# Writing the exponentials of a tile's second part in place in SBUF instead of into a PSUM bank

## The chip, the core and the metric

The kernel runs on one core of one Trainium2 chip. The metric is the device time of one execution in microseconds. Three runs of the kernel before gave 1191.39, 1193.56 and 1194.45 us; the median is 1193.56 us. Lower is better.

## What is computed

The program is a two-layer decoder trunk on 1024 tokens of width 1024. Only the second layer's main branch matters here: attention with a forget gate, 16 heads of width 64, causal, over keys and values that are projected once. In the reference, cut to what matters:

```python
logits = jnp.einsum('bqhd,bkhd->bhqk', qi, k) * scale
logits = logits + (ci[..., :, None] - cum_k[:, :, None, :])
logits = jnp.where(mask[None, None], logits, -jnp.inf)
p = jax.nn.softmax(logits, axis=-1)
return jnp.einsum('bhqk,bkhd->bqhd', p.astype(v.dtype), v)
```

The queries go through in blocks of 128. `cum` is the running sum of the log forget gates; in the kernel it comes as a row `R` that is added to the logits.

## The kernel before

The stage is `fox`. It runs 16 heads one after the other (head 0 to head 15), and in each head eight tiles of 128 queries, the longest first: tile 7 has 1024 keys, tile 0 has 128. A tile with more than 512 keys goes in two parts: 512+512 (tile 7), 512+384 (tile 6), 512+256 (tile 5), 384+256 (tile 4). Tiles 3 to 0 have one part.

The texts below use one letter for each step of a tile, with the tile's number and `a` or `b` for its part. All of it stands in `probs`, `inverse_of` and `halves`:

- **The logits**: two TensorE matmuls (L323) into a PSUM bank of tag `L`, of which there are three.
- **R**: the VectorE reduction on L1028. It reads the `L` bank, adds the row, writes the sum to the SBUF tile `p` (tag `MK`, four slots) and keeps the running minimum. When it has read the bank, the matmuls may use that bank again.
- **E**: the exponential on ScalarE (L1036). It reads `p`, writes `e`, and gives the row's sum. Its bias is the minimum over both parts, so E of part `a` too must wait until R of part `b` is done.
- **S** and **V**: the sum of the parts' sums (L1046, or L1048 for one part) and its reciprocal (L1049), on VectorE.
- **C**: on ScalarE (L1064), `e` times the reciprocal, rounded to float16, into the tile `P`.
- **H**: on VectorE (L1065), the rest that the rounding left: `e` times the reciprocal minus C's result, into the other half of `P`.

The two halves are then transposed by a DMA (L1081) and meet the values on TensorE (L1090) six tiles later. C and H of a tile are written in the program behind the first R of the next tile.

`e` lies in a PSUM bank of tag `T`. There are two such banks, and in the kernel before each part of a tile takes one. So a tile of two parts takes both, and E of the next tile waits for H of this one.

Between these steps run pieces of the projections for the coming heads: matmuls on L359, which fill most of TensorE's time, and their evacuations, which share VectorE and ScalarE with the steps above (L912 and L913 queries and keys, L816 and L817 values, L375 and L376 gates, L1107 and L1108 the output of the values). GpSimd adds the causal mask to the row (L1002) and scales and splits the projection weights (L176, L193, L178). During heads 14 and 15 the weights of the output projection are split too (L198 on ScalarE, L199 on VectorE, L193 on GpSimd).

TensorE's order is the program's order, fixed by hand. The order on VectorE and ScalarE is made by the scheduler from what each instruction needs and from which slots are free; so is most of GpSimd's and of the DMA queue's.

Of the kernel before, what the change touches and what calls it, by code (L numbers as in the profile page):

```python
# [18 lines left out]
P = 128  # L19
# [4 lines left out]
NH = 512  # L24
# [54 lines left out]
def trunk_kernel(ctx, tc, x, xT, memT, win, wk, wv0, wv, wmk, wmv, wout, poolw, pscale, lng, lnb, bforget, out):  # L79
# [20 lines left out]
    def nm(tag):  # L100
        count[0] += 1
        return f"{tag}{count[0]}"
# [4 lines left out]
    def ps(shape, tag, bufs):  # L107
        return psum.tile(shape, F32, tag=tag, name=nm(tag), bufs=bufs)
# [7 lines left out]
    def MK(shape, dt=F32R):  # L116
        return sb(list(shape), "MK", 4, dt)
# [7 lines left out]
    def tiny(n, dt=F32):  # L125
        return small.tile([P, n], dt, tag=f"s{n}{dt}", name=nm("s"), bufs=4 if n < 12 else 2)
# [193 lines left out]
    def mm3(acc, terms):  # L320

        for i, (a, b) in enumerate(terms):
            nc.tensor.matmul(acc, a, b, start=i == 0, stop=i == len(terms) - 1)  # L323
# [137 lines left out]
    def mem_attention(l, X, kv, qtile, ytile, yd, behind=None, before=None, last=None):  # L461
# [61 lines left out]
        with tc.manual_schedule(engines={PE}):  # L523
            for t in range(ST + 2):
                part = fill.left / (ST + 2 - t)
                if t < ST:
                    probs(t)
                if before and t == ST - 2:
                    before()
                if last and t == ST:  # L530
                    last(0)
                at = (0.3, 0, 0.1, 0.6) if t in (5, 9) else (1, 0, 0, 0)
                for h in range(MH):
                    fill.pump(part * at[h])
                    if t in (5, 9):
                        values((t - 5) // 4, h)
            fill.pump(float("inf"))
# [258 lines left out]
    with tc.tile_pool(name="in1", bufs=1) as in1:  # L796
# [194 lines left out]
        def parts_at(i):  # L991

            L = (i + 1) * P
            return [(0, L)] if L <= NH else [(0, 384), (384, L)] if L == 640 else [(0, NH), (NH, L)]
# [17 lines left out]
        def probs(hd, i, R, sums, inverse, behind):  # L1012

            q, kx, ky = pairs[hd // 2][hd % 2]
            qs = slice(i * P, (i + 1) * P)
            p = MK([P, S], F32)  # L1020
            C, parts = diagonal.pop((hd, i)), parts_at(i)
            m = tiny(2)
            top = -NEG
            for n, (lo, up) in enumerate(parts):
                lg = ps([P, NH], "L", 3)[:, : up - lo]
                mm3(lg, ((q[:, qs], kx[:, lo:up]), (q[:, qs], ky[:, lo:up])))
                rows = C[:, : up - lo] if n == len(parts) - 1 else R[:, lo:up]
                nc.vector.tensor_tensor_reduce(p[:, lo:up], lg, rows, unq, top, ALU.add, ALU.min, m[:, n : n + 1])  # L1028
                top = m[:, n : n + 1]
                if n == 0:  # L1030
                    inverse()
            behind()
            es = []
            for n, (lo, up) in enumerate(parts):
                e = ps([P, NH], "T", 2)[:, : up - lo]
                nc.scalar.activation(  # L1036
                    e, p[:, lo:up], AF.Exp, bias=top, scale=-1.0, accum_out=sums[:, n, hd % 2, i : i + 1],
                )
                es.append((lo, up, e))
            return hd, i, es, sums  # L1040
# [92 lines left out]
        def fox(following, out_proj, head):  # L1133
# [8 lines left out]
            for hd in range(HEADS + 1):  # L1142
# [16 lines left out]
                for i in range(ST if hd < HEADS else LAG):  # L1159
# [37 lines left out]
                    if hd < HEADS:  # L1197
                        new = (hd, tile_of, o)
                        fresh[0] = probs(hd, tile_of, R, sums, inverse, behind)
                    else:  # L1200
                        inverse()
                        behind()
                        out_proj.split(11 + i, True, gp_copy)
                        if i > 1:
                            out_proj.fetch_two(two_lines(4 + 2 * i))
# [91 lines left out]
```

## Time and profile before

| | |
|---|---|
| the profiled execution, its own time | 1193.68 us |
| its span, first to last instruction | 1192.0 us |
| median of the runs | 1193.56 us (1191.39 to 1194.45) |
| mean granted TensorE clock | 0.998 |
| stage of the 16 heads | about 645 to 1055 us of the span |
| VectorE, ScalarE, GpSimd busy in the whole span | 783.0, 684.9, 286.0 us |

The span is what the trace covers; 1.68 us of the profiled execution lie around it. A row of the timeline gives the start, the duration, the engine, the line and the operation, then what is written and read with sizes; a bracket at the end gives how long the engine had sat idle and what ended that. A row with x2 or more stands for so many instructions, and its shape is the first one's. Busy times and waits are averages over very different stretches, so the trace is read here head by head.

### The profile page before, as it was taken

What the parts mean: (1) busy time and instruction counts of PE and PEld (TensorE: products, weight loads), DVE (VectorE), ACT (ScalarE), POOL (GpSimd) and SP (SyncE); (2) the same over time, 40 slices, a digit from 0 to 9 for tenths busy, and PEclk for the clock granted to TensorE, in tenths of its full rate; (3) what the DMA queues carried; (4) which work ended last, traced back from release to release, by engine and by line L of the source; (5) the groups of instructions that cost most, each with busy time, mean ns of one, the idle gap of its engine ahead of it and who ended that gap; (6) DMA issues with size and microseconds to landing.
All of it is one profiled execution on the core that took longest, in us unless ns stands there. A gap on an engine that the chain in (4) does not pass through costs nothing. (4 is left out here: it accounts for less than half of the span.)

```text
span 1192.0 us, 19788 instructions
## 1 busy us (share of the span) xinstructions
PE 1164.5 (98%) x6893; PEld 672.4 (56%) x6941; DVE 783.0 (66%) x1840; ACT 684.9 (57%) x1512; POOL 286.0 (24%) x437
## 2 busy tenths in 40 slices
PE   9999999999999999999999999999999999999996
PEld 5566776555555557556574555555555545455553
DVE  6744675555765566447655888778877788884654
ACT  6568775966563234557431776666766677674210
POOL 3321001310000000000002454555555444750000
PEclk9999999999999999999999999999999999999999
DMA  7576656754286544446634889989996899964530
GB/s 258 179 237 194 162 113 213 239 182 145 91 281 174 144 133 119 140 130 124 173 150 113 173 183 218 192 170 201 193 216 145 167 193 208 238 164 171 176 108 35
DMA packets 286195, 203.88 MB, mean 171 GB/s; under 512 B 224912, under 2 KB 238352, under 8 KB 286096
## 3 DMA queue, kind: packets, MB, share of 16 engines
q1 hardware_dynamic: 279696, 181.59, 60.9%
q0 software_dynamic: 6400, 21.04, 5.4%
q8 instruction: 54, 0.88, 0.3%
q14 instruction: 45, 0.37, 0.1%
HBM read 116.01 MB, written 22.61 MB: 116 GB/s over the span
## 5 line engine op out<-in xcount | busy, mean ns | idle before, releaser
L359 PE MATMUL pj<-A,w 128*128 128x512 f16 (+2 forms) x2874 | 660.8, 382 | 3.3 <-DMA A<-A 0.9
L359 PEld LDWEIGHTS <-w 128*128 128x128 f16 (+1 forms) x2560 | 245.5, 98 | 278.4 <-issue 9.9
L1036 ACT ACTIVATE T<-MK,s 128x512 f32<-128x512 f32 x192 | 111.2, 579 | 66.0 <-DVE s L1028 48.8
L1065 DVE SCALAR_TENSOR_TENSOR P<-T,s,P 128x512 f16<-128x512 f32 x192 | 112.0, 613 | 39.4 <-ACT P L1064 38.3
L1064 ACT ACTIVATE P<-T,s 128x512 f16<-128x512 f32 x192 | 102.9, 576 | 53.5 <-issue 28.9
L599 PEld LDWEIGHTS <-T 128*128 128x128 bf16 x736 | 70.6, 98 | 89.5 <-issue 4.4
L1002 POOL TENSOR_SCALAR_AFFINE_SELECT raw<-R 128x256 f32<-128x256 f32 (+3 forms) x128 | 59.8, 469 | 185.5 <-DVE s L1028 102.8
L323 PE MATMUL L<-A 128*128 128x512 f16 (+3 forms) x384 | 84.7, 326 | 5.5 <-DVE s L1028 5.4
L199 DVE TENSOR_TENSOR w<-raw,w 128x512 bf16<-128x512 f32 x74 | 51.8, 701 | 54.1 <-ACT w L198 38.8
L885 POOL MEMSET G<- 128x128 f32 x1 | 0.2, 204 | 335.2 <-DVE V L541 335.2
L359 PEld LDWEIGHTS pj<-A,w 128*128 128x128 f32 x352 | 65.2, 188 | 16.9 <-ACT w L198 1.5
L199 DVE TENSOR_TENSOR T<-T,T 128x1024 bf16<-128x1024 f32 x23 | 28.1, 1220 | 71.0 <-PE pj L599 37.9
L323 PEld LDWEIGHTS <-A 128*128 128x128 f16 x384 | 37.4, 98 | 48.9 <-issue 7.6
L178 POOL TENSOR_TENSOR w<-B,w 128x512 f16<-128x512 f32 x54 | 63.2, 1172 | 4.0
L198 ACT CAST T<-T 128x1024 fp32r<-128x1024 f32 x23 | 24.1, 1047 | 64.7 <-DMA T<-y1d 34.6
L198 ACT CAST w<-raw 128x512 fp32r<-128x512 f32 x76 | 46.7, 615 | 23.8 <-DMA raw<-in_win_dram 10.7
L1090 PEld LDWEIGHTS <-V 128*64 128x64 f16 (+1 forms) x1152 | 50.6, 104 | 13.3 <-issue 5.6
L1090 PE MATMUL O<-T,V 128*64 128x128 f16 (+1 forms) x1152 | 57.5, 220 | 0.4 <-ACT T L1036 0.4
L599 PE MATMUL pj<-B,T 128*128 128x512 bf16 (+1 forms) x187 | 52.1, 385 | 0.3
L1028 DVE CUSTOM_DVE_ANT_0 MK<-L,R,scales 128x512 f32<-128x512 f32 x64 | 45.3, 708 | 9.7 <-PE L L323 9.3
L200 ACT CAST w<-raw 128x512 bf16<-128x512 f32 x78 | 48.2, 618 | 5.7 <-PE pj L359 4.3
L599 PE MATMUL L<-B,T 128*128 128x512 bf16 (+1 forms) x165 | 46.9, 394 | 0.4 <-ACT T L200 0.2
(286 smaller groups left out, 1845.7 us busy)
## 6 DMA issues: line engine op xcount, KB each, us to landing
raw<-in_win_dram SPq DMA_DIRECT2D x66, 256.0 KB, 3.5
W<-in_win_dram POOLq DMA_DIRECT2D x48, 256.0 KB, 4.1
R<-cumd SPq DMA_DIRECT2D x16, 512.0 KB, 4.5
B<-in_win_dram SPq DMA_DIRECT2D x15, 512.0 KB, 5.1
y0d<-Y SPq DMA_DIRECT2D x12, 512.0 KB, 4.2
raw<-in_wout_dram SPq DMA_DIRECT2D x24, 256.0 KB, 2.7
T<-y0d SPq DMA_DIRECT2D x12, 512.0 KB, 4.9
A<-A SPq DMA_DIRECT2D x24, 256.0 KB, 3.9
```

The costliest lines, as they stand in the source:

```text
L178: pin(nc.gpsimd.tensor_tensor(to.lo, src, to.hi, ALU.subtract))
L198: pin(nc.scalar.copy(to.hi, src))
L199: pin(nc.vector.tensor_tensor(to.lo, src, to.hi.bitcast(F32), ALU.subtract))
L200: pin((top or nc.scalar.copy)(to.top, src))
L323: nc.tensor.matmul(acc, a, b, start=i == 0, stop=i == len(terms) - 1)
L359: nc.tensor.matmul(accs[n], a[:, k, :], b[:, pc * 4 + k, n * NH : (n + 1) * NH], start=seen[n] == 1, stop=seen[n] == 3 * KT,)
L599: nc.tensor.matmul(accs[a][nh], y, w, start=kt == 8 and i == 0, stop=kt == 7 and i == 2,)
L1002: tc.keep_in_program_order(nc.gpsimd.affine_select(C[:, :w], R[:, lo:up], [[-1, w]], ALU.is_ge, -NEG, base=w - P, channel_multiplier=1,))
L1036: nc.scalar.activation(e, p[:, lo:up], AF.Exp, bias=top, scale=-1.0, accum_out=sums[:, n, hd % 2, i : i + 1],)
L1064: nc.scalar.activation(pair[:, lo:up], e, AF.Copy, scale=r)
L1065: nc.vector.scalar_tensor_tensor(pair[:, L + lo : L + up], e, r, pair[:, lo:up], ALU.mult, ALU.subtract)
L1090: nc.tensor.matmul(acc[rows, (i % 4) * P : (i % 4) * P + P], v[:, b, 2 * j : 2 * j + (1 if e else 2), :].rearrange("p e d -> p (e d)"), pt ...
```

## The change

`e` of a tile's first part still goes into a `T` bank; `e` of the second part is written over `p` in SBUF:

```diff
             es = []
             for n, (lo, up) in enumerate(parts):
-                e = ps([P, NH], "T", 2)[:, : up - lo]
+                e = p[:, lo:up] if n else ps([P, NH], "T", 2)[:, : up - lo]
                 nc.scalar.activation(
                     e, p[:, lo:up], AF.Exp, bias=top, scale=-1.0, accum_out=sums[:, n, hd % 2, i : i + 1],
                 )
```

No instruction is added or removed. For the four tiles of two parts in each head, 64 in all, E of part `b` writes SBUF, and C and H of part `b` read SBUF. A tile now takes one `T` bank, and `p` stays in use until H of its part `b`. TensorE's rows are the same ones in the same order. On ScalarE and VectorE the scheduler makes another order.

ScalarE at the start of head 7, before. The tile `p` is `MK_8938` for tile 7 and `MK_8981` for tile 6; L1036 is E, L1064 is C, L1107 evacuates the output of the values:

```order
L1036 ACTIVATE T_8953,sums_8561<-MK_8938,s_8939 128x512
L1036 ACTIVATE T_8955,sums_8561<-MK_8938,s_8939 128x512
L1064 ACTIVATE P_8994<-T_8953,s_8987 128x512
L1064 ACTIVATE P_8994<-T_8955,s_8987 128x512
L1107 ACTIVATE G_8560<-O_9005,scales 64x512
L1036 ACTIVATE T_8999,sums_8561<-MK_8981,s_8982 128x512
L1036 ACTIVATE T_9001,sums_8561<-MK_8981,s_8982 128x384
```

The same place with the change (`p` is `MK_8910` for tile 7, `MK_8952` for tile 6, `MK_9037` for tile 5):

```order
L1036 ACTIVATE T_8925,sums_8537<-MK_8910,s_8911 128x512
L1036 ACTIVATE MK_8910,sums_8537<-MK_8910,s_8911 128x512
L1036 ACTIVATE T_8970,sums_8537<-MK_8952,s_8953 128x512
L1064 ACTIVATE P_8965<-T_8925,s_8958 128x512
L1064 ACTIVATE P_8965<-MK_8910,s_8958 128x512
L1036 ACTIVATE MK_8952,sums_8537<-MK_8952,s_8953 128x384
L1107 ACTIVATE G_8536<-O_8975,scales 64x512
L1036 ACTIVATE T_9055,sums_8537<-MK_9037,s_9038 128x512
```

E6a has moved ahead of C7a and C7b, and E5a stands right behind L1107. Heads 0 to 3, 6, 7 and 10 to 13 have this order with the change; heads 4, 5, 8, 9, 14 and 15 keep E7a, E7b, C7a, C7b, E6a.

VectorE a little later in head 7, before (L1065 is H of tile 7, then L1108, R5a, S6, R5b):

```order
L1065 TENSOR_SCALAR P_8994<-T_8953,s_8987,P_8994 128x512
L1065 TENSOR_SCALAR P_8994<-T_8955,s_8987,P_8994 128x512
L1108 TENSOR_SCALAR G_8560<-O_9005,scales,G_8560 64x512
L1028 ISA MK_9067,s_9068<-L_9069,R_8601,scales 128x512
L1046 TENSOR_SCALAR s_9073<-sums_8561 128x1
L1028 ISA MK_9067,s_9068<-L_9076,raw_8900,s_9068,scales 128x256
```

And with the change:

```order
L1065 TENSOR_SCALAR P_8965<-T_8925,s_8958,P_8965 128x512
L1065 TENSOR_SCALAR P_8965<-MK_8910,s_8958,P_8965 128x512
L1028 ISA MK_9037,s_9038<-L_9039,R_8576,scales 128x512
L1108 TENSOR_SCALAR G_8536<-O_8975,scales,G_8536 64x512
L1046 TENSOR_SCALAR s_9043<-sums_8537 128x1
L1028 ISA MK_9037,s_9038<-L_9046,raw_8872,s_9038,scales 128x256
```

R5a and L1108 have changed places, and H7b reads two SBUF tiles (`MK` and `P`) where it read a PSUM bank and one SBUF tile.

VectorE at the start of head 14, before (R7a, L817, R7b, then H0a of head 13, R6a, S7, R6b, V7):

```order
L1028 ISA MK_11591,s_11592<-L_11600,raw_11464,s_11592,scales 128x512
L1065 TENSOR_SCALAR P_11561<-T_11564,s_11597,P_11561 128x128
L1028 ISA MK_11639,s_11640<-L_11641,R_11255,scales 128x512
L1046 TENSOR_SCALAR s_11645<-sums_11583 128x1
L1028 ISA MK_11639,s_11640<-L_11648,raw_11519,s_11640,scales 128x384
L1049 RECIPROCAL s_11645<-s_11645 128x1
```

And with the change:

```order
L1028 ISA MK_11535,s_11536<-L_11544,raw_11408,s_11536,scales 128x512
L1046 TENSOR_SCALAR s_11588<-sums_11527 128x1
L1049 RECIPROCAL s_11588<-s_11588 128x1
L1028 ISA MK_11582,s_11583<-L_11584,R_11202,scales 128x512
L1065 TENSOR_SCALAR P_11595<-T_11550,s_11588,P_11595 128x512
L1028 ISA MK_11582,s_11583<-L_11591,raw_11463,s_11583,scales 128x384
```

R6a now stands behind S7 and V7, and R6b behind H7a; H0a of the head before has gone ahead of R7a. Heads 4 and 8 change in the same way; heads 5, 9 and 15 had this order already.

## The prediction

> **What bounds the kernel now.** I read the page's first part, then the busy time of the stage of the 16 heads as one stretch, then who waited for whom in that stretch, TensorE first. The rows are:
>
> ```profile
> PE 1164.5 (98%) x6893; PEld 672.4 (56%) x6941; DVE 783.0 (66%) x1840; ACT 684.9 (57%) x1512; POOL 286.0 (24%) x437
> 640.00:1060.00 420.00, 414.10 (x2886) 218.55 (x2886) 327.48 (x937) 286.53 (x681) 217.94 (x327) 1.00 0.91 191
> PE L L323 <- DVE s L1028: 5.4, 8, 2.1
> PE O L1090 <- ACT T L1036: 0.4, 1, 0.4
> DVE P L1065 <- ACT P L1064: 38.3, 61, 1.1
> DVE MK L1028 <- PE L L323: 9.3, 7, 4.3
> ACT T L1036 <- DVE P L1065: 16.6, 42, 0.8
> ```
>
> The second row has, behind the 420 us, the busy times of TensorE, its weight loads, VectorE, ScalarE and GpSimd. TensorE is busy for 414.1 of 420 us, so the whole stage holds 5.9 us that could be won: eight waits of logits matmuls for R (5.4 us) and one at the values (0.4). VectorE has 22% idle, but the waits say what kind: it stands for ScalarE's C (38.3 us) and almost never for TensorE (9.3 us in only 7 places). VectorE and ScalarE hand each tile back and forth, R, E, S, V, C, H, and this loop, not their busy time, runs close behind TensorE. The wait that the change removes, E for H's bank, is 16.6 us of ScalarE's time. It costs TensorE only where it makes an R late.
>
> The eight places, one row each from the timeline:
>
> ```profile
> 702.68 0.38 PE L323 MATMUL L<-A 128*128 128x256 f16 x2 [0.23 <-DVE s L1028]
> 726.07 0.38 PE L323 MATMUL L<-A 128*128 128x256 f16 x2 [0.54 <-DVE s L1028]
> 828.67 0.38 PE L323 MATMUL L<-A 128*128 128x256 f16 x2 [0.44 <-DVE s L1028]
> 931.27 0.38 PE L323 MATMUL L<-A 128*128 128x256 f16 x2 [0.45 <-DVE s L1028]
> 971.44 0.48 PE L323 MATMUL L<-A 128*128 128x384 f16 x2 [0.26 <-DVE s L1028]
> 978.80 0.38 PE L323 MATMUL L<-A 128*128 128x256 f16 x2 [1.12 <-DVE s L1028]
> 1024.82 0.48 PE L323 MATMUL L<-A 128*128 128x384 f16 x2 [0.30 <-DVE s L1028]
> 1034.41 0.38 PE L323 MATMUL L<-A 128*128 128x256 f16 x2 [2.05 <-DVE s L1028]
> ```
>
> The 256-wide ones are the logits of tile 4, part b, in heads 2, 3, 7, 11, 13 and 15; they need the bank that R5a frees, three banks back. The 384-wide ones are those of tile 6, part b, in heads 13 and 15, and need R7a.
>
> **The new order, walked through head 7.** I take durations from the trace and the new order from the rows shown with the change.
>
> ```profile
> 820.51 0.74 DVE L1028 CUSTOM_DVE_ANT_0 MK<-L,R,scales 128x512 f32<-128x512 f32 x1
> 822.62 0.69 ACT L1036 ACTIVATE T<-MK,s 128x512 f32<-128x512 f32 x1 [1.93 <-DVE s L1028]
> 823.34 0.67 ACT L1036 ACTIVATE T<-MK,s 128x512 f32<-128x512 f32 x1
> 824.18 0.21 DVE L1046 TENSOR_SCALAR s<-sums 128x1 f32<-128x1 f32 x1 [0.92 <-ACT T L1036]
> 824.33 0.68 DVE L1028 CUSTOM_DVE_ANT_0 MK<-L,raw,s 128x384 f32<-128x384 f32 x1
> 824.93 0.16 DVE L1049 RECIPROCAL s<-s 128x1 f32<-128x1 f32 x1
> 825.17 1.26 ACT L1064 ACTIVATE P<-T,s 128x512 f16<-128x512 f32 x2 [1.03 <-issue]
> 825.89 1.41 DVE L1065 SCALAR_TENSOR_TENSOR P<-T,s,P 128x512 f16<-128x512 f32 x2 [0.80 <-ACT P L1064]
> 827.22 0.73 DVE L1108 SCALAR_TENSOR_TENSOR G<-O,scales,G 64x512 f32<-64x512 f32 x1
> 827.88 0.73 DVE L1028 CUSTOM_DVE_ANT_0 MK<-L,R,scales 128x512 f32<-128x512 f32 x1
> ```
>
> Before: R6b ends at 825.01, C7a starts at 825.17, H7a 0.72 later, both H take 1.41, L1108 follows, and R5a ends at 828.61; TensorE goes on at 828.67. With the change ScalarE has E6a ahead of C7a, and E6a needs the minimum that R6b completes: it starts at 825.05, and since one E follows another after 0.72 (822.62 to 823.34), C7a starts at 825.77 instead of 825.17. H7a starts at 825.77 + 0.72 = 826.49, both H are over at 827.90, and R5a, which no longer stands behind L1108, runs from 827.82 (neighbours overlap by 0.07) to 828.55. So at this place the change gives 0.66 (L1108 out of the way) and takes 0.60 (E6a in the way): **0.06 us, nearly nothing**. ScalarE's wait for the bank is gone, and TensorE's stall here stays, unless the head starts earlier.
>
> The gain comes later in the head, from tile 4:
>
> ```profile
> 834.23 1.14 DVE L1065 SCALAR_TENSOR_TENSOR P<-T,s,P 128x512 f16<-128x512 f32 x2 [0.80 <-ACT P L1064]
> 835.01 0.58 ACT L1036 ACTIVATE T<-MK,s 128x384 f32<-128x384 f32 x1 [0.45 <-DVE P L1065]
> 837.35 1.01 DVE L1065 SCALAR_TENSOR_TENSOR P<-T,s,P 128x384 f16<-128x384 f32 x2 [0.70 <-ACT P L1064]
> 843.90 0.74 DVE L1028 CUSTOM_DVE_ANT_0 MK<-L,R,scales 128x512 f32<-128x512 f32 x1
> 818.32 1.03 PE L323 MATMUL L<-A 128*128 128x512 f16 x4
> 841.83 1.03 PE L323 MATMUL L<-A 128*128 128x512 f16 x4
> ```
>
> E4a waited here until H5a gave its bank back (835.01). With the change that bank was freed by H6a, and E4a stands behind E5b, at about 832.3; S4 is then ready before H5a, and H4a can start at about 836.6, 0.75 earlier. Of this the next head keeps some 0.45, since H0a (about 0.3) now stands ahead of its R7a: R7a of head 8 at about 843.45, not 843.90. One turn of the loop takes 22.95 us instead of the 23.39 from 820.51 to 843.90. TensorE's own turn is 841.83 - 818.32 = 23.51 with its stall of 0.44, so 23.1 without.
>
> **The cost of reading SBUF.** The moved operations have no row before; the nearest ones:
>
> ```profile
> L1065 DVE SCALAR_TENSOR_TENSOR P<-T,s,P 128x512 f16<-128x512 f32 x80 | 58.8, 748 | 28.9 <-ACT P L1064 27.9
> L172 DVE SCALAR_TENSOR_TENSOR w<-raw,scales,w 128x512 f16<-128x512 f32 x22 | 16.2, 748 | 9.5 <-ACT w L171 9.4
> L504 ACT ACTIVATE P<-P,s 128x256 f16<-128x256 f32 x64 | 27.3, 497 | 3.7 <-ACT P L498 2.6 <-DVE s L502 1.0
> L1064 ACT ACTIVATE P<-T,s 128x256 f16<-128x256 f32 x48 | 22.3, 465 | 2.9 <-ACT T L1036 2.8
> L199 DVE TENSOR_TENSOR MK<-raw,MK 128x512 bf16<-128x512 f32 x8 | 5.5, 688 | 9.6 <-ACT MK L198 9.5
> L199 DVE TENSOR_TENSOR MK<-A,MK 128x512 bf16<-128x512 f32 x4 | 4.3, 1091 | 0.1
> ```
>
> H by itself costs the same: 748 ns with a PSUM and an SBUF input, 748 ns with two SBUF inputs (L172). C costs 32 ns more from SBUF (497 against 465), 64 times on ScalarE, 2 us in all beside idle time. E into SBUF I take as free. But L199, with two SBUF inputs, takes 688 ns early and 1091 ns in head 14 and behind it, where GpSimd is busier: up to 0.40 us more. H of part b becomes such an instruction, while GpSimd is busy for 217.94 of 420 us, 52%. So one H costs between 0 and 0.40 more; I take 0.52 x 0.40 = 0.2, four times a head, 0.8, and let half of it vanish in VectorE's waits, which remain. The turn is then 22.95 + 0.4 = 23.35, against 23.39 before in head 7: at the middle of the bounds the price eats what the order gives.
>
> The Trainium skill speaks against the change here: SBUF — State Buffer, section "Who interferes with whom", says that a VectorE instruction with two SBUF inputs and a GpSimd one that reads SBUF block each other, while one with a single SBUF input does not contend. The 688 and 1091 ns of L199 agree; by a full block at every H the sum would come out as in the second rival below. The skill's Perfetto Trace Analysis, section "Optimizing Scalar/DVE Operations", puts VectorE's access at some 60 ns from SBUF and 125 ns from PSUM; by that H would be 65 ns cheaper, which the equal 748 ns do not show.
>
> **The sum.** Against the profiled execution, 1193.68 us, of which 1192.0 is span. What the loop's turn is worth shows best where heads of the new order follow each other:
>
> ```profile
> 898.64 0.75 DVE L1028 CUSTOM_DVE_ANT_0 MK<-L,R,scales 128x512 f32<-128x512 f32 x1 [0.68 <-PE L L323]
> 970.63 0.74 DVE L1028 CUSTOM_DVE_ANT_0 MK<-L,R,scales 128x512 f32<-128x512 f32 x1
> ```
>
> These are R7a of heads 10 and 13: 72.0 us for three heads, 24.0 each. At 23.35, plus 0.35 in head 10, which starts up to date and waits for TensorE's tiles, it is 70.4, so head 13 starts 1.6 earlier. TensorE itself comes 0.45 earlier (head 11's stall), so 1.15 of head 13's 0.26 + 1.12 goes. Head 6 starts up to date as well, so heads 7 and 11 lose their 0.44 and 0.45. Of heads 2 and 3 (0.23 + 0.54) I take 0.5. Head 15 keeps its 0.30 + 2.05: its order is the old one up to tile 4, and head 14 ahead of it gets the order R7b, S7, V7, R6a, in which R5a comes about 2 us later (R6a, 0.66, no longer fills VectorE's wait for E7b, and S6, which waits for E6a and E6b, 1.5, stands ahead of R5a). For that order in heads 4, 8 and 14 I set 0.3 of new stalls. Gain: 0.44 + 0.45 + 1.15 + 0.5 - 0.3 = 2.2 us. The execution would take 1191.5; the median of the runs lies 0.12 below the profiled one, so **1191.3 us**.
>
> **The rivals.**
>
> *The loop loosens everywhere.* Head 14 and 15 profit too and the eight waits all go. For it: 16.6 us of E's waits fall away, three times what TensorE loses. Against it: the orders of heads 14 and 15. The ceiling is 5.9 us: 1193.56 - 5.8 = 1187.8.
>
> *GpSimd's hold on SBUF decides.* H of part b costs the full 0.40 each and half or all of it lands in the loop, 0.8 to 1.6 a head: turns of 23.75 to 24.55 against TensorE's 23.1. In the ten heads of the new order TensorE would lose 0.65 to 1.45 a head, less some 1.2 that a run of heads starts with in hand (R7a of head 7 came 820.51 - 818.32 = 2.2 behind its logits and stalled 0.44; a head that is up to date has about 0.6), three runs: 6.5 - 3.6 = 3 to 14.5 - 3.6 = 11, and 1.5 more in heads 14 and 15. With head 15's 2.35 and the 0.4, the stalls are 7 to 15 instead of 5.9: 1195 to 1203, nearest 1197. It decides from about 0.15 us an H that is not absorbed.
>
> *Given back at the end.* Heads 2 to 13 gain 2.2, and the later R5a of head 14 makes head 15 start 2 us later: 1193.5.
>
> That the change does not do what it says is excluded by the order: 64 E write the `MK` tile. The longer life of `p` costs no wait: even where only two of its four slots are left, in head 15, R of a tile stands behind H of the tile two before it in VectorE's own order.
>
> **Chances.** The forecast has 0.38, its own range 1189.6 to 1192.8. All waits gone, 0.20; GpSimd decides, 0.30; given back, 0.12. For 8 in 10 the range runs from 1187.6 to 1197.6: it holds the forecast, the ceiling and the nearer half of the GpSimd rival. 0.3% of the time is 3.6 us, about what a measurement of this kernel can tell from no change. Faster by more (below 1190.0): 0.10 of the forecast and the whole first rival, 0.30. Slower by more (above 1197.1): 0.25 of the GpSimd rival and 0.02 of the last, 0.27. Within: 0.43.
>
> **What would show it.** Right: E no longer waits for L1065; the 256-wide waits of heads 7, 11 and 13 shrink below 0.3 while head 15's stays near 2; H of part b (P<-MK) 0.1 to 0.3 us longer than H of part a at 512. Wrong: H of part b at 1.0 us or more; TensorE's waits for R above 6 us in sum; C7a not delayed by E6a; TensorE's waits for R below 1 us.

## The result and the profile after

The changed kernel takes 1196.84 us (median of six runs, 1195.68 to 1198.35), the kernel before 1193.13 (six runs, 1191.23 to 1194.45). The ratio is 1.0033, with a 95% interval of 1.0020 to 1.0047: **slower by about 3.7 us**, where 2.2 us less had been forecast. The profiled execution took 1198.35 us, with a span of 1196.6.

The page's first part, and the busy times of the stage of the 16 heads (TensorE, its weight loads, VectorE, ScalarE, GpSimd), after:

```profile
PE 1169.4 (98%) x6941; PEld 672.3 (56%) x6941; DVE 788.0 (66%) x1840; ACT 685.3 (57%) x1512; POOL 294.6 (25%) x437
640.00:1060.00 420.00, 412.78 (x2876) 217.01 (x2874) 328.81 (x933) 285.38 (x678) 222.28 (x323) 1.00 0.90 188
```

VectorE and GpSimd are each some 5 to 9 us busier over the span with the same instructions. Who waited for whom in the stage, after:

```profile
ACT T L1036 <- DVE P L1065: 3.8, 11, 1.0
ACT T L1036 <- DVE s L1028: 97.2, 86, 2.7
DVE P L1065 <- ACT P L1064: 35.9, 56, 1.4
PE L L323 <- DVE s L1028: 4.8, 8, 1.1
PE L L323 <- DVE s L1049: 1.7, 2, 1.2
```

E's wait for the bank that H frees has shrunk from 16.6 to 3.8 us, as meant. It bought nothing: E waits for R instead, 97.2 us where it was 48.8. TensorE's waits for R are 4.8 us against 5.4, and a wait of another kind is new (1.7 us, logits that start a head). The profile puts it down to a V (L1049); `e1` and `e12` below, in which the moves of the queries come earlier, are without it. The places of the timeline where TensorE stood idle in the stage and right behind it (two of 0.38 and 0.34 us for evacuations left out), after:

```profile
704.21 0.38 PE L323 MATMUL L<-A 128*128 128x256 f16 x2 [1.05 <-DVE s L1028]
727.69 0.38 PE L323 MATMUL L<-A 128*128 128x256 f16 x2 [0.49 <-DVE s L1028]
807.51 0.38 PE L323 MATMUL L<-A 128*128 128x256 f16 x2 [0.23 <-DVE s L1028]
830.99 0.38 PE L323 MATMUL L<-A 128*128 128x256 f16 x2 [0.49 <-DVE s L1028]
845.49 1.02 PE L323 MATMUL L<-A 128*128 128x512 f16 x4 [1.18 <-DVE s L1049]
935.10 0.38 PE L323 MATMUL L<-A 128*128 128x256 f16 x2 [0.49 <-DVE s L1028]
959.26 0.38 PE L323 MATMUL L<-A 128*128 128x256 f16 x2 [0.87 <-DVE s L1028]
983.14 0.38 PE L323 MATMUL L<-A 128*128 128x256 f16 x2 [0.49 <-DVE s L1028]
996.94 1.02 PE L323 MATMUL L<-A 128*128 128x512 f16 x4 [0.48 <-DVE s L1049]
1037.60 0.38 PE L323 MATMUL L<-A 128*128 128x256 f16 x2 [0.72 <-DVE s L1028]
1069.80 0.60 PE L599 MATMUL L<-B,T 128*128 128x512 bf16 x2 [0.88 <-ACT T L200]
```

These are heads 2, 3, 6, 7, the first logits of head 8, heads 11, 12, 13, the first logits of head 14, head 15, and the output projection. Heads 6 and 12 and the two first logits are new, head 2 has grown from 0.23 to 1.05, heads 13 and 15 have shrunk. How far the changed kernel lags, from the starts of the same matmuls in both profiles:

| place | before | after | lag, us |
|---|---|---|---|
| first logits of head 0 | 649.29 | 650.68 | 1.39 |
| logits of tile 4, part b, head 2 | 702.68 | 704.21 | 1.53 |
| first logits of head 8 | 841.83 | 845.49 | 3.66 |
| first logits of head 14 | 991.96 | 996.94 | 4.98 |
| logits of tile 4, part b, head 15 | 1034.41 | 1037.60 | 3.19 |
| output projection, first stored rows | 1065.18 | 1069.80 | 4.62 |
| end of the span | 1192.0 | 1196.6 | 4.6 |

The first 1.39 us stand ahead of the stage, where no order differs; the granted clock was 0.97 in the first 100 us of this execution, 1.00 in that of before. From the first logits on the loss is 3.2 us. It arises in three kinds of place: ahead of tile 4's logits, at the start of heads 8 and 14, and between the last logits and the output projection (the lag goes from 3.19 to 4.62); in heads 14 and 15 the changed kernel makes up 1.8 us in between. What H costs, by shape, after:

```profile
L1065 DVE SCALAR_TENSOR_TENSOR P<-T,s,P 128x512 f16<-128x512 f32 x64 | 48.0, 750 | 31.0 <-ACT P L1064 30.1
L1065 DVE SCALAR_TENSOR_TENSOR P<-MK,s,P 128x512 f16<-128x512 f32 x16 | 15.4, 964 | 0.0
L1065 DVE SCALAR_TENSOR_TENSOR P<-MK,s,P 128x384 f16<-128x384 f32 x16 | 11.1, 695 | 0.0
L1065 DVE SCALAR_TENSOR_TENSOR P<-MK,s,P 128x256 f16<-128x256 f32 x32 | 18.6, 581 | 0.0
```

At 512 a part b (`P<-MK`) costs 214 ns more than a part a; with 80 more at 384 (against 615 from PSUM) and 100 at 256 (481), the 64 of them cost 16 x 0.214 + 16 x 0.080 + 32 x 0.100 = 7.9 us more. The mean hides what matters. Head 12, VectorE, GpSimd and TensorE, after:

```profile
956.83 1.16 POOL L178 TENSOR_TENSOR w<-B,w 128x512 f16<-128x512 f32 x1
956.91 1.62 DVE L1065 SCALAR_TENSOR_TENSOR P<-MK,s,P 128x512 f16<-128x512 f32 x1
958.46 0.74 DVE L1028 CUSTOM_DVE_ANT_0 MK<-L,R,scales 128x512 f32<-128x512 f32 x1
959.26 0.38 PE L323 MATMUL L<-A 128*128 128x256 f16 x2 [0.87 <-DVE s L1028]
```

GpSimd's subtraction of the weight split (L178) starts 0.08 us ahead of H7b. H7b then takes 1.62 us instead of 0.75 and ends behind it, R5a follows, and TensorE waits 0.87 us for R5a's bank. Exactly this, with 1.62 us each time, stands at H7b of heads 2, 6, 10 and 12 (701.87, 805.18, 909.28, 956.91). Eleven other H of part b are held too, by 0.25 to 0.68 us, but none of them is H7b; the remaining 49 take at most 0.06 us more than is usual for their shape.

The other kind, in head 7. ScalarE and then the DMA queue (SPq), after:

```profile
830.06 0.69 ACT L1107 ACTIVATE G<-O,scales 64x512 f32<-64x512 f32 x1
832.21 0.69 ACT L1036 ACTIVATE T<-MK,s 128x512 f32<-128x512 f32 x1 [1.46 <-DVE s L1028]
836.68 0.58 ACT L912 ACTIVATE A<-pj 128x512 f16<-128x512 f32 x1
836.20 2.96 SPq L1081 DMA_TRANSPOSE T<-P  x1
839.21 0.58 SPq L909 DMA_DIRECT2D A<-A  x1
839.90 1.46 SPq L1081 DMA_TRANSPOSE T<-P  x1
841.46 1.64 SPq L909 DMA_DIRECT2D A<-A  x2
```

And the same two in the kernel before:

```profile
830.55 0.60 ACT L912 ACTIVATE A<-pj 128x512 f16<-128x512 f32 x1
835.75 1.22 SPq L909 DMA_DIRECT2D A<-A  x2
```

Before, L912, which evacuates the last queries for head 8, ran ahead of E5a, since E5a still had no bank. Now E5a, E5b, E4a, E4b, C5a and C5b stand ahead of it, though ScalarE sits idle for 1.46 us in front of E5a. L912 comes 6.1 us later (lag included), and the last two moves of the queries between partitions (L909) come 5.7 us later, among the transposes. Head 8's first logits start at 845.49, 2.4 behind the last move's issue, after an idle time of 1.18.

### The profile page after: what moved, and what is told of

It is laid out like the page before. It is cut to its first block, busy times and chain, and to the rows that moved or that the text cites. A ratio compares the mean times of both kernels' runs of the same rounds, so it can differ in the third digit from the quotient of the medians.

```text
span 1196.6 us, 19828 instructions
## 1 busy us (share of the span) xinstructions
PE 1169.4 (98%) x6941; PEld 672.3 (56%) x6941; DVE 788.0 (66%) x1840; ACT 685.3 (57%) x1512; POOL 294.6 (25%) x437
## 5 line engine op out<-in xcount | busy, mean ns | idle before, releaser
L1036 ACT ACTIVATE T<-MK,s 128x512 f32<-128x512 f32 (+3 forms) x128 | 76.3, 596 | 101.1 <-DVE s L1028 97.2
L1002 POOL TENSOR_SCALAR_AFFINE_SELECT raw<-R 128x256 f32<-128x256 f32 (+3 forms) x128 | 65.6, 515 | 176.0 <-DVE s L1028 111.0
L1065 DVE SCALAR_TENSOR_TENSOR P<-T,s,P 128x512 f16<-128x512 f32 (+3 forms) x128 | 80.8, 632 | 38.4 <-ACT P L1064 35.9
L199 DVE TENSOR_TENSOR w<-raw,w 128x512 bf16<-128x512 f32 x74 | 51.9, 701 | 55.4 <-ACT w L198 40.4
L1064 ACT ACTIVATE P<-T,s 128x512 f16<-128x512 f32 (+3 forms) x128 | 74.8, 586 | 22.3 <-ACT T L1036 7.5
L199 DVE TENSOR_TENSOR T<-T,T 128x1024 bf16<-128x1024 f32 x23 | 28.1, 1220 | 68.9 <-PE pj L599 37.6
L178 POOL TENSOR_TENSOR w<-B,w 128x512 f16<-128x512 f32 x54 | 64.7, 1198 | 3.7
```

The lines of the kernel that those rows point to most:

```text
L178: pin(nc.gpsimd.tensor_tensor(to.lo, src, to.hi, ALU.subtract))
L199: pin(nc.vector.tensor_tensor(to.lo, src, to.hi.bitcast(F32), ALU.subtract))
L1002: tc.keep_in_program_order(nc.gpsimd.affine_select(C[:, :w], R[:, lo:up], [[-1, w]], ALU.is_ge, -NEG, base=w - P, channel_multiplier=1,))
L1036: nc.scalar.activation(e, p[:, lo:up], AF.Exp, bias=top, scale=-1.0, accum_out=sums[:, n, hd % 2, i : i + 1],)
L1064: nc.scalar.activation(pair[:, lo:up], e, AF.Copy, scale=r)
L1065: nc.vector.scalar_tensor_tensor(pair[:, L + lo : L + up], e, r, pair[:, lo:up], ALU.mult, ALU.subtract)
```

## The experiments

Three theories: **price and collision** (H with two SBUF inputs is dearer, or stands behind GpSimd at places that count), **evacuation and queue** (queries and their moves come too late), and **order** in general. An order was imposed on the program by edges between instructions of one engine, which say only who is issued first:

```diff
         trunk_kernel(tc, *args)
+        follow(tc, ORDERS)
...
+def follow(tc, orders):
...
+        for before, after in zip(row, row[1:]):
+            tc.add_manual_dep(
+                after, before.name,
+                mybir.DependencyInfo(mybir.DependencyClass.NoSync, mybir.DependencyReason.DATA), reason="order",
+            )
```

`ORDERS` holds, for each engine named, the order of one of the two kernels. All ratios are to the kernel before, run beside it. One more figure is given for each run, from its one profiled execution: the time from the first logits of head 0 to the end of the span, 542.7 us in the kernel before and 545.9 in the changed one. It leaves out what lies ahead of the stage, where no order was changed and the executions still took between 645.9 and 651.2 us; being a single execution, it has no interval.

**1 to 4: order and place taken apart.** `e1` is the changed kernel with the DMA queue's old order; `e2` with the old order everywhere; `e3` is the kernel before with the new order of the DMA queue; `e4` is `e2` with part a in place too:

```diff
-                e = p[:, lo:up] if n else ps([P, NH], "T", 2)[:, : up - lo]
+                e = p[:, lo:up] if n or len(parts) == 2 else ps([P, NH], "T", 2)[:, : up - lo]
```

> The changed kernel, with only the DMA queue's order put back to that of the kernel before: the moves of queries and keys (L909) stand ahead of the transposes (L1081) and of the row's load (L1009) again; VectorE, ScalarE and GpSimd keep the new order. Queue theory (the late moves hold up the first logits of heads 8 and 14, 1.53 + 0.83 us by the weight loads' starts): those two waits go, 1196.8 - 2.4 = 1194.4. Price theory (H of part b is dearer with two SBUF inputs): stays at 1196.8. Order theory (the new order on VectorE and ScalarE costs): 1196.8.

> E of part b still written in place, but VectorE, ScalarE and the DMA queue in the exact order of the kernel before, GpSimd too but for two neighbours. What is left is the price of the place alone. Queue and order theories: 1193.1 to 1193.6, as before. Price theory: 64 H at 0.08 to 0.21 us more and 64 C at 0.03 more lengthen the loop R, E, S, V, C, H: 1196 or above, the R-waits of TensorE above 7 us.

> The kernel before, with only the DMA queue's order taken from the changed kernel; E of both parts in PSUM, VectorE and ScalarE as before. Queue theory: the first logits of heads 8 and 14 wait, 1193.1 + 2.4 = 1195.5. Price and order theories: 1193.1.

> E of part a too in place for tiles of two parts, so 128 H read two SBUF inputs instead of 64, in the order of the kernel before on VectorE, ScalarE and the DMA queue. It doubles the price of the place at an unchanged order. Price theory: twice the difference of the run with part b alone in that order, 1199 or above. Queue and order theories: within 1 us of that run, 1193 to 1194.5.

| run | median, us | ratio, 95% interval | first logits to end, us |
|---|---|---|---|
| e1, only the queue's old order | 1196.46 | 1.0026 (1.0011 to 1.0041) | 545.9 |
| e2, place alone, old order | 1192.16 | 0.9999 (0.9987 to 1.0010) | 542.2 |
| e3, new queue order alone | 1194.56 | 1.0020 (1.0010 to 1.0029) | 543.1 |
| e4, 128 H from SBUF, old order | 1202.70 | 1.0090 (1.0075 to 1.0105) | 553.0 |

`e2` is the central one: the edit itself, in the old order, costs nothing that the runs show, though H is as dear as in the changed kernel. H of part b there, and in `e4`:

```profile
L1065 DVE SCALAR_TENSOR_TENSOR P<-MK,s,P 128x512 f16<-128x512 f32 x16 | 14.0, 877 | 0.0
L1065 DVE SCALAR_TENSOR_TENSOR P<-MK,s,P 128x256 f16<-128x256 f32 x32 | 20.9, 652 | 0.0
```
```profile
L1065 DVE SCALAR_TENSOR_TENSOR P<-MK,s,P 128x512 f16<-128x512 f32 x64 | 54.2, 863 | 28.1 <-ACT P L1064 28.1
PE L L323 <- DVE s L1028: 10.9, 9, 2.5
```

16 x 0.13 + 16 x 0.01 + 32 x 0.17 is 7.7 us more in `e2`, almost the 7.9 of the changed kernel. So the price is the same and what it costs depends on where it falls. One H7b is still held for nearly the whole of L178, in head 2, and TensorE waits there for 1.19 us (0.23 in the kernel before); heads 7 and 11 no longer wait. From `e2`:

```profile
696.57 1.67 DVE L1065 SCALAR_TENSOR_TENSOR P<-MK,s,P 128x512 f16<-128x512 f32 x1
699.87 0.38 PE L323 MATMUL L<-A 128*128 128x256 f16 x2 [1.19 <-DVE s L1028]
```

With 128 such H (`e4`) the time is 10 us longer, where the price theory had put twice what `e2` loses, and TensorE's waits for R are twice the 5.4 of before; E and C of part a write and read SBUF there too, so this is not the price of H alone. `e3` is slower than the kernel before, by 1.8 us in the medians, but not as expected: the first logits of head 8 do not wait, those of head 14 wait for 0.37 us, and from the first logits of head 0 on its profiled execution is only 0.4 us longer. Where the new queue order costs time is not shown. `e1` missed: the moves are back ahead of the transposes, and the queries are now in time, but they are evacuated so late that the queue stands still in front of the moves, and the transposes behind them come late. TensorE waits for those instead, up to 1.87 us:

```profile
PE O L1090 <- DMA T<-P: 4.2, 4, 1.9
952.68 2.47 PE L1090 MATMUL O<-T,V 128*64 128x128 f16 x52 [1.87 <-DMA T<-P]
```

**5 to 8: the evacuation, the queue, the end, another bank.** `e5` puts priority on L912 and L913, `e6` issues the moves on GpSimd's queue, `e7` has the old order from head 15 on, `e8` gives every fourth part's logits a `T` bank:

```diff
-            nc.scalar.activation(hi[:, cols], acc, AF.Copy, scale=factor)
+            with tc.high_priority(): nc.scalar.activation(hi[:, cols], acc, AF.Copy, scale=factor)
```
```diff
-                nc.sync.dma_start(to[rows, :], of[old, :])
+                nc.gpsimd.dma_start(to[rows, :], of[old, :])
```
```diff
-                lg = ps([P, NH], "L", 3)[:, : up - lo]
+                lg = ps([P, NH], *(("T", 2) if nth[0] % 4 == 3 else ("L", 3)))[:, : up - lo]; nth[0] += 1
```

> The changed kernel, with priority in the scheduler for the evacuation of queries and keys (L912 on ScalarE, L913 on VectorE). In heads 7 and 13 L912 then stands behind C6a, where the changed kernel has it behind C5b, five instructions and a wait for R5b later. Evacuation theory (what now runs ahead on ScalarE, E5a, E4a, C5a, delays the queries by 3.8 us, so their moves come late or the transposes behind them do): the waits of the first logits of heads 8 and 14 go, 1196.8 - 2.4 = 1194.4. Price theory and loop theory (the turn R, E, S, V, C, H alone is longer): 1196.8.

> The changed kernel with the moves (L909) issued from GpSimd's queue; the orders of VectorE and ScalarE are those of the changed kernel to the row. Evacuation theory in its queue form (L913 of the last queries ends at 838.2, the moves wait behind transposes until 841.5 to 843.1): the moves go at about 838.5 without holding up a transpose, the first logits of heads 8 and 14 do not wait, 1194.4. If the late evacuation is too late by itself: 1196 or more. Price theory: 1196.8 or more, since GpSimd gets more to do.

> The changed kernel with the order of the kernel before from head 15 on alone (VectorE, ScalarE, GpSimd, DMA queue). In the profiles TensorE loses 1.47 us between the last logits and the output projection (0.67 + 0.80), but gains 1.8 in head 15 against the kernel before. Order theory: both are given back, 1196.8 - 1.5 + 1.8, about 1197; tail alone 1195.3. Price theory: 1196.8.

> The changed kernel, with every fourth part's logits in a T bank, so that logits have four banks and E of the first part shares the two T banks with them. If the waits of logits for R are what the stage still loses (4.8 us in the changed kernel), they fall below 1: 1193. If the loss is in the evacuation and the queue: 1196 or more. The turn R, E, S, V, C, H stays as long as it is, E waits for H's bank again.

| run | median, us | ratio, 95% interval | first logits to end, us |
|---|---|---|---|
| e5 | 1202.39 | 1.0081 (1.0066 to 1.0096) | 551.5 |
| e6 | 1217.02 | 1.0202 (1.0182 to 1.0222) | 568.1 |
| e7 | 1195.94 | 1.0025 (1.0016 to 1.0034) | 545.5 |
| e8 | 1242.95 | 1.0418 (1.0402 to 1.0434) | 593.4 |

Three of the four missed widely. In `e5` the first logits of heads 8 and 14 no longer wait, as expected, but TensorE's waits for R go from 4.8 to 12.7 us: the priority sets L912 between C6a and C6b, in the middle of the turn. `e6` tells nothing of the moves by themselves, since GpSimd now stands for them (30.8 us for earlier moves to land, and more for L912 and L913) with the masks and splits queued behind. `e7` gains 0.9 of the 1.5 that the end loses, which its interval does not separate from nothing: the output projection no longer waits, but head 15's wait for R is 1.62 us instead of 0.72. `e8` turned E's wait into TensorE's: logits in a `T` bank wait for the H that used it before. The waits in `e5` and in `e8`:

```profile
PE L L323 <- DVE s L1028: 12.7, 15, 1.9
```
```profile
PE T L323 <- DVE P L1065: 34.6, 14, 3.8
```

**9: the four collisions alone.** Every order stays; L178 waits for H7b in heads 2, 6, 10 and 12 (the pairs are places in VectorE's and GpSimd's program order):

```diff
+    for first, then in [(882, 143), (1064, 225), (1246, 303), (1336, 339)]:
+        tc.add_manual_dep(
+            pool[then], vector[first].name,
+            mybir.DependencyInfo(mybir.DependencyClass.Sync, mybir.DependencyReason.DATA), reason="order",
+        )
```

> The changed kernel with four waits more and every order unchanged: in heads 2, 6, 10 and 12 the weight split on GpSimd (L178) that started together with H7b waits until H7b is done. In the changed kernel these four H7b take 1.62 us, until L178 is over, where H7b beside no L178 takes 0.75, and R5a stands right behind. Collision theory: the four H7b take 0.75, R5a comes 0.87 earlier, the waits of logits in heads 2, 6 and 12 (+0.82, +0.40, +1.04 against the kernel before) go: 1196.8 - 2.3 = 1194.5. Evacuation theory alone: 1196.8. If R5a, which also reads a row from SBUF, is held in H's place: 1196.8.

1193.70 us, ratio 1.0005 (0.9993 to 1.0016): **3.1 of the 3.7 us are gone**, more than the 2.3 expected. From the first logits of head 0 to the end the profiled execution takes 543.4 us, which is 2.5 less than in the changed kernel. The place in head 12, and who waited in this kernel:

```profile
950.72 0.74 DVE L1065 SCALAR_TENSOR_TENSOR P<-MK,s,P 128x512 f16<-128x512 f32 x1
951.38 0.75 DVE L1028 CUSTOM_DVE_ANT_0 MK<-L,R,scales 128x512 f32<-128x512 f32 x1
951.61 1.16 POOL L178 TENSOR_TENSOR w<-B,w 128x512 f16<-128x512 f32 x1 [1.05 <-DVE P L1065]
PE L L323 <- DVE s L1028: 2.7, 5, 1.3
840.15 1.02 PE L323 MATMUL L<-A 128*128 128x512 f16 x4 [1.35 <-DMA A<-A]
```

H7b takes 0.74, and GpSimd waits 1.05 instead. The waits for R in heads 6, 7, 11 and 12 are gone: heads 7 and 11 had waited only because heads 6 and 10 handed their 0.87 on. The wait at head 8 is 1.35 us instead of 1.18, and the profile now puts it down to the moves. The eleven other held H are still held here (H6b of head 12 takes 1.29 us, H4b of heads 3, 7, 11 and 13 each 0.88 or 0.89), and the time is that of the kernel before all the same.

**10 and 11: late queries without the change, and a fourth bank.** `e10` is the kernel before with edges that set L912 and L913 behind the same neighbours as in the changed kernel. `e11` keeps the old order, and frees a whole bank (in it the `T` banks are two tags, `TA` and `TB`, and the program's other uses of `T` take them in turn):

```diff
-                e = p[:, lo:up] if n else ps([P, NH], "T", 2)[:, : up - lo]
+                e = p[:, lo:up] if n or i in (2, 0) else ps([P, NH], "TA", 1)[:, : up - lo]
...
-                lg = ps([P, NH], "L", 3)[:, : up - lo]
+                lg = ps([P, NH], *(("TB", 1) if nth[0] % 4 == 3 else ("L", 3)))[:, : up - lo]; nth[0] += 1
```

> The kernel before, E of both parts in PSUM, with the evacuation of queries and keys alone (L912, L913) set behind the same C, E, H or R as in the changed kernel: in heads 7 and 13 L912 stands behind C5b, no longer ahead of E5a. Evacuation theory: the first logits of heads 8 and 14 wait, about 2.4 us, less what R gains where L912 no longer stands in front of E5a: 1193.5 to 1195. Collision theory: no H reads two SBUF inputs, so 1192.5 as before.

> The place of the change used otherwise: E of part b in place, E of tiles 2 and 0 in place too, so that E needs one T bank instead of two; the other T bank goes to the logits as a fourth bank. VectorE, ScalarE and the DMA queue in the order of the kernel before. If what TensorE still waits for in the order of the kernel before is the bank that R frees three parts back (4.8 us), these waits fall below 1: 1187.5 to 1188.5. If the turn R, E, S, V, C, H is as long as TensorE's, the waits only come later: 1191 to 1192.5.

`e10`: 1196.86, 1.0026 (1.0015 to 1.0036). It loses as much as the change does, but not where it was expected: the first logits of head 8 wait for 0.31 us and those of head 14 not at all, while the waits for R rose from 5.4 to 8.1. The scheduler also moved other rows with L912, so this is no clean price of late queries. `e11`: 1196.49, 1.0019 (1.0006 to 1.0032). No wait for R is left in the stage, and yet the kernel is slower than the one before: TensorE runs ahead and waits for evacuations instead, among them these:

```profile
PE pj L359 <- DVE MK L817: 3.3, 3, 1.6
PE pj L359 <- POOL w L193: 1.1, 1, 1.1
```

**12 to 14: the queries moved with nothing else.** `e12` is the changed kernel with its own order kept, but L912 ahead of E5a, in ScalarE's idle 1.46 us, and L913 behind H6b. `e13` adds the four waits of `e9`; `e14` adds the old order from head 15 on.

> The changed kernel in its own order on VectorE and ScalarE, with only the evacuation of the last queries (and of keys and the other queries where it stands behind C5b) moved: L912 from behind C5b to ahead of E5a, where ScalarE stands idle for R5b (1.46 us in head 7), L913 from behind H5b to behind H6b. The four collisions of H7b stay. Evacuation theory: the first logits of heads 8 and 14 do not wait (2.4 us), nothing on the turn R, E, S, V, C, H is put off by more than 0.7: 1194.5. Collision theory: the other part, 3.1, stays: 1196.8 if the queries cost nothing by themselves.

> Both at once: the evacuation moved as in the run before this, and the four waits that keep L178 behind H7b in heads 2, 6, 10 and 12 (which alone gave 1193.7). If both causes add up: 1193.7 - 2.4 = 1191.3, faster than the kernel before. If one hides the other: 1193.7.

> As the run before this, and from head 15 on in the order of the kernel before (which alone gave 0.9). If the three add up: 1190.4. If the tail's gain is lost to the wait in head 15: as the run before this.

| run | median, us | ratio, 95% interval | first logits to end, us |
|---|---|---|---|
| e12 | 1196.54 | 1.0027 (1.0014 to 1.0040) | 545.8 |
| e13 | 1192.07 | 0.9990 (0.9979 to 1.0002) | 543.2 |
| e14 | 1194.82 | 1.0002 (0.9986 to 1.0017) | 543.3 |

In `e12` the waits at the first logits of heads 8 and 14 are gone, and the time is the same as in the changed kernel: TensorE's waits for R are 7.6 instead of 4.8 us. With the collisions in place, what TensorE does not lose to the queries it loses to R a few tiles later. With them out (`e13`) the same move is worth 1.6 us against `e9` by the medians, but the intervals overlap, and from the first logits of head 0 to the end the two profiled executions are equally long (543.2 and 543.4 us). A gain from it is not shown. `e13` has the lowest median among the versions with the order of the change, and no run shows it, or any other, faster than the kernel before beyond the interval. `e14` shows no gain on top of `e13`: the output projection no longer waits, but head 15's wait for R is 2.22 us, and the two are equally long.

## Why the prediction was wrong

**What held.** E no longer waits for L1065 (3.8 us in place of 16.6), and E6a goes ahead of C7a. In head 7 the walk met the trace: C7a at 828.15 is 0.72 behind E6a, R5a runs ahead of L1108, the stall stays at 0.49, and R7a to R7a is 846.18 - 822.90 = 23.28 us, forecast 23.35. The price was well sized as a mean: 214 ns at 512, 0.12 us over all 64 where 0.2 was taken. Half of that vanishing was even too cautious: `e2` loses nothing.

**The step that failed** is in the part on the price: "I take 0.52 x 0.40 = 0.2, four times a head, 0.8, and let half of it vanish". A share of GpSimd's busy time was made into an even cost for every H. But the collisions do not spread evenly: 15 of the 64 are held, and at places that recur (H7b in heads 2, 6, 10 and 12, H4b in heads 3, 7, 11 and 13). H7b stands directly ahead of R5a, the R for whose bank TensorE waits, and in four heads it met L178 at its start and took 0.87 more, over twice the upper bound of 0.40. That bound was the mean of four L199, which took from 0.69 to 1.26 us. The trace of the kernel before held one meeting of the full size, in head 14, which a mean by group does not show. An L199 with two SBUF inputs starts 0.07 us behind L178 and takes 1.64 us, where the same one takes 0.68 beside nothing:

```profile
1010.38 1.16 POOL L178 TENSOR_TENSOR w<-B,w 128x512 f16<-128x512 f32 x1
1010.45 1.64 DVE L199 TENSOR_TENSOR B<-B,B 128x512 bf16<-128x512 f32 x1
```

`e9` removes the four at H7b alone and gets 3.1 us back. Without them heads 7 and 11 lose their stalls, just as the sum had it (0.44 + 0.45); with them heads 6 and 10 are not "up to date" and hand the delay on.

**Of the sum's other terms** the 1.15 of head 13 came as 0.89 (1.12 + 0.26 to 0.49), and head 15, set to keep its 2.35, lost 1.63 of it. Heads 2 and 3, set to gain 0.5, lost 0.77 (0.23 + 0.54 to 1.05 + 0.49), with a collision in head 2. Of the signs that were set, the waits of heads 7, 11 and 13 did not fall below 0.3 (0.49 each), and head 15's 256-wide one did not stay near 2 (0.72).

**What was left out**: the walk followed R, E, S, V, C and H, and neither L912 nor the DMA queue behind it. E's wait for the bank was not idle time. In the kernel before it was the gap in which ScalarE evacuated the queries, and filling it with E5a to C5b pushed them back by more than 3 us beyond the lag. The two waits that this makes, at heads 8 and 14, were in no row of the prediction; removing them changed nothing beside the collisions (`e12`), and without the collisions no gain is shown (`e13`). The new wait of 0.88 at the output projection was in no row either. It is gone where the old order holds from head 15 on (`e7`, `e14`), but there head 15 waits longer, so what the end costs stays open.

**The rivals.** "GpSimd's hold on SBUF decides", nearest 1197, is what happened, 1196.84, by the mechanism named but not by its working: not 0.8 to 1.6 us in every head, but 0.87 in four. That its number came so close is luck. Its point of decision, 0.15 us an H that is not absorbed, was the wrong measure, since the mean was below it. "The loop loosens everywhere" is ruled out as far as the place goes: even with no wait for R left (`e11`) the time did not fall.

## What to carry to other kernels

A cost that comes from two engines meeting is not a mean: list the places where the pair can start together, and ask at each who waits directly behind; four meetings of 0.87 us decided here, while the other sixty instructions of the same kind, some 4.4 us longer in sum, stay as they are in `e9`, which is no slower than the kernel before within its interval. Look for such meetings row by row: a mean over a group of instructions hides them. When a wait is removed, look at what ran in it: the instructions that used the gap are pushed back, and so are the queue entries that they release. To tell an edit's own price from that of the order it brings, impose the old order on the new data placement; here that one run separated them.

## What the runs showed of the hardware

In the two pairs shown here the instruction that started later was held, for most of what the other had left. With L178 0.08 us ahead, H7b took 1.62 us (above): 0.87 more, where L178 had 1.08 left. With H6b of head 2 ahead by 0.26 us, H6b kept the time that it has beside nothing, and L178 took 1.37 instead of 1.16, 0.21 more, where H6b had 0.35 left:

```profile
707.99 0.61 DVE L1065 SCALAR_TENSOR_TENSOR P<-MK,s,P 128x384 f16<-128x384 f32 x1
708.25 1.37 POOL L178 TENSOR_TENSOR w<-B,w 128x512 f16<-128x512 f32 x1
```

So an H can also cost GpSimd: it was 222.28 us busy in the stage, 217.94 before. With one SBUF input, as in the kernel before, no H was held. H over the whole run, before (a PSUM bank and one SBUF tile) and after (two SBUF tiles), with the least, the median and the longest in ns:

```profile
L1065 DVE SCALAR_TENSOR_TENSOR P<-T,s,P x192: 339/610/753, 655.5 to 1053.7; 128x512 f16<-128x512 f32 x80, 128x384 f16<-128x384 f32 x48, 128x256 f16<-128x256 f32 x48, 128x128 f16<-128x128 f32 x16
```
```profile
L1065 DVE SCALAR_TENSOR_TENSOR P<-MK,s,P x64: 470/610/1620, 658.1 to 1047.1; 128x256 f16<-128x256 f32 x32, 128x512 f16<-128x512 f32 x16, 128x384 f16<-128x384 f32 x16
```

The longest of 192 was 753 ns, the longest of 64 now is 1620. The Trainium skill, SBUF — State Buffer, section "Who interferes with whom", says that the order of issue decides who blocks, not the kind of instruction, and that a VectorE instruction with at most one SBUF input, outside the two-port modes, does not contend with GpSimd. The trace agrees with both: 0.87 us one way and 0.21 the other, and no H above 753 ns with one. Where the starts lie closer the trace is no proof of the order: in heads 5 and 9, H5b starts 0.02 us ahead of an L193 and still takes 0.90 us instead of 0.48, and times on GpSimd are rough.
